# Rotating images by 90 degrees: the last four slabs turned in pairs, and a new order of stores

## Chip, cores, metric

One Trainium2 chip, one core. The metric is device time in microseconds (us) of one execution, the median of several runs. "Faster" or "slower" is said of differences over 2%; this study is about differences of a few tenths of a per cent, so each kernel is compared with runs of the kernel before on the same chip, with a 95% interval.

## The reference

```python
def setup_inputs():
    batch, c, h, w = 32, 3, 256, 256
    return {"x": np.random.randn(batch, c, h, w).astype(np.float32)}

def reference(x):
    return np.rot90(x, k=-1, axes=(-2, -1)).astype(np.float32)
```

96 images of 256x256 floats: 25.17 MB are read and 25.17 MB written, with no arithmetic.

## The kernel before

The images are cut into 12 slabs of 2.097 MB (8 images each), and a slab fills one unit of 16 KB in each of the 128 partitions. All slabs are loaded, turned by VectorE in 32x32 blocks, and stored when the loads are over. Slab n is turned into the unit that slab n-1 has left; slab 0 goes to PSUM and is copied back by ScalarE (ACT) at the end.

A slab that is turned alone has long rows (16 KB, 16 image rows, as one DMA packet) on one of its two sides only. `short` and `long` are the two cuts of the image rows:

```python
    def short(rows):
        return rows.rearrange("(n i p r) w -> n p i (r w)", i=I, p=P, r=RS)        # RS = 8: 8 KB runs

    def long(rows):
        return rows.rearrange("(n i m r) w -> n i m (r w)", i=I, m=P // I, r=RL)   # RL = 16: 16 KB runs
    ...
    long_st = (0, 1, 2, last)          # loaded in 8 KB, stored in 16 KB; the others the other way round
    for n in range(n_slabs):           # loads
        if n in (1, 2):
            ld = nc.sync.dma_start(out=units[n], in_=ld_short[n])
            continue
        for i in range(I):
            if n in long_st:
                ld = nc.sync.dma_start(out=units[n][:, i], in_=ld_short[n][:, i])
            else:
                ld = nc.sync.dma_start(out=units[n][i::I].rearrange("p i f -> p (i f)"), in_=ld_long[n, i])
            if (n, i) == (last, 0):
                mark = ld              # the first store waits for this load
    ...
    for n in range(n_slabs):           # turn, then store
        t_in, t_out = units[n], units[n - 1] if n else turned0
        ...                            # two transposes of 128x2048 elements
        if n in range(5, last):
            nc.sync.dma_start(out=st_short[n], in_=t_out)         # 2 MB, 256 packets of 8 KB
        elif n:
            for i in range(I):
                st = store(n, t_out, i)                           # 1 MB each
                ...
```

## Time and profile before

| | before |
|---|---|
| median, 3 runs | 123.8 us (123.74 to 123.87) |
| span of the profiled run | 121.9 us |
| VectorE busy | 92.9 us (76%) |
| DMA queue | 5248 packets (4608 of data), 98.1% busy |

The span is what the profiler sees between the first and the last instruction; the time of a run is about 1.9 us longer. The lines of the profile that carry this are shown in the prediction. Beside the page and its views I use the packet records of the trace: start, duration and bytes of every DMA packet. In the records a packet and the next one on its engine overlap, mostly by 3 or 4 ns.

### The profile page before, as it was taken

The page shows a single profiled execution, that of the slowest core. Times are in us where ns is not written, and L with a number is a line of the kernel's source. Part 1 is how long each engine was busy: PE and PEld are TensorE (multiplying, and loading weights), DVE is VectorE, ACT ScalarE, POOL GpSimd, SP SyncE. Part 2 cuts the span into 40 slices and gives each one's busy share as a digit, 9 for nine tenths or more (in the row PEclk, how much of TensorE's full clock was granted, in tenths as well). Part 3 has the DMA queues.
Part 4 walks back from the last instruction along what each step waited for, and adds up shares of the span by engine and source line. Part 5 has one row for each costly group of instructions (what it writes and reads, how often), then busy time and mean ns, then how long its engine had stood idle before and what let it go on. Part 6 is the DMA issues. An engine that isn't in the chain of part 4 may idle for free.

```text
span 121.9 us, 137 instructions
## 1 busy us (share of the span) xinstructions
DVE 92.9 (76%) x24; ACT 4.9 (4%) x3; POOL 0.2 (0%) x4
## 2 busy tenths in 40 slices
DVE  0039999999999999999999999999999992000000
ACT  0000000000000000000400000000000007400000
POOL 0000000000000000000000000000000000000000
DMA  3999999999999999999999999999999999999994
GB/s 86 430 430 430 427 433 430 430 430 430 430 430 430 430 430 430 430 430 390 427 468 430 430 390 430 430 430 430 411 419 419 427 419 419 414 427 473 425 419 188
DMA packets 5248, 50.33 MB, mean 413 GB/s; under 512 B 640, under 2 KB 640, under 8 KB 640
## 3 DMA queue, kind: packets, MB, share of 16 engines
q1 hardware_dynamic: 5248, 50.33, 98.1%
HBM read 25.17 MB, written 25.17 MB: 413 GB/s over the span
## 4 chain that ended last, share of the span: by engine, by line
DVE 44%; issue 29%; DMA 6%; DVEq 3%; ACT 2%; ACTq 1%; SPq 0%
DVE u L98 26%; DVE u L92 12%; DVE turned L92 6%; DMA u<-in_x_dram 6%; DVEq L138 3%; ACT u L110 2%; ACTq L138 1%; SPq L73 0%; DVEq L92 0%
## 5 line engine op out<-in xcount | busy, mean ns | idle before, releaser
L98 DVE STREAM_TRANSPOSE u<-u 128x2048 f32<-128x2048 f32 x16 | 62.4, 3947 | 0.3
L92 DVE STREAM_TRANSPOSE u<-u 128x2048 f32<-128x2048 f32 x6 | 23.4, 3984 | 0.1
L92 DVE STREAM_TRANSPOSE turned<-u 128x2048 f32<-128x2048 f32 x2 | 7.1, 3586 | 8.1 <-DMA u<-in_x_dram 8.1
L110 ACT COPY u<-turned 128x2048 f32<-128x2048 f32 x2 | 3.6, 1869 | 40.5 <-DVE u L92 40.5
L110 ACT ACT_TABLE_LOAD x1 | 1.3, 1283 | 59.6 <-DMA u<-in_x_dram 59.6
L127 POOL MEMSET const-bfloat16-1.0<- 128x1 bf16 x1 | 0.1, 102 | 0.0
L127 POOL MEMSET const-uint8-127<- 128x1 uint8 x1 | 0.1, 102 | 0.0
L127 POOL MEMSET const-float32-0.0<- 128x1 f32 x1 | 0.1, 99 | 0.2 <-issue 0.2
L127 POOL MEMSET const-float32-1.0<- 128x1 f32 x1 | 0.1, 99 | 0.0
## 6 DMA issues: line engine op xcount, KB each, us to landing
u<-in_x_dram SPq DMA_DIRECT2D x20, 1024.0 KB, 19.6
out_dram<-u SPq DMA_DIRECT2D x12, 1024.0 KB, 12.1
out_dram<-u SPq DMA_DIRECT2D x6, 2048.0 KB, 20.9
u<-in_x_dram SPq DMA_DIRECT2D x2, 2048.0 KB, 13.5
```

The lines of the kernel that those rows point to most:

```text
L92: nc.vector.transpose(out=dst[:, cs], in_=src[:, cs])
L98: nc.vector.transpose(out=dst[:, cs], in_=src[:, cs])
L110: nc.scalar.copy(out=units[last][:, i], in_=turned0[:, i])
L127: nc = _bacc.Bacc("TRN2", target_bir_lowering=False, num_devices=1)
L138: with _tile.TileContext(nc) as tc:
```

## The change

Its intent: a slab alone can have 16 KB packets on one side only, but two slabs that are turned together can have them on both. Slabs 8 and 9, and 10 and 11, become such pairs. A pair needs two free units at once, so stores must have left one by then: the stores of slabs 3 to 7 come first (4 at the very front, because the pair 8/9 goes into the units of slabs 3 and 7), then 1 and 2, then the pairs. Cut to its core:

```diff
-    long_st = (0, 1, 2, last)
+    long_st = (0, 1, 2)
+    both = (8, 10)
+    adjacent = [(3, 7), (8, 9), (10, 11)]          # units that lie side by side in one tile
...
-    for n in range(n_slabs):
+    for n in (0, 1, 2, 3, 7, 4, 5, 6, *range(8, n_slabs)):          # loads
...
+        elif n in paired:
+            src = pairs[both.index(n) + 1].rearrange("p a (r g c) -> p c r g a", r=RL, c=RL)
+            dst = pairs[both.index(n)].rearrange("p i (c k r) -> p c r k i", c=RL, r=RL)[:, :, ::-1, ::-1, :]
+            parts, step = 4, RL // 4
...
+        if n in paired:
+            for i in range(I):
+                nc.sync.dma_start(out=st_long[n, i], in_=pairs[both.index(first)][n - first :: I, i])
...
-        if n in range(5, last):
-            nc.sync.dma_start(out=st_short[n], in_=t_out)
+            return nc.sync.dma_start(out=st_short[n], in_=fours(home[n]))     # slabs 3 to 7, 2 MB each
...
+    for n in range(both[0]):
+        turn(n)
+    for n in (4, 3, 5, 6, 7, 1, 2):
+        st = store(n)
+    for n in range(both[0], n_slabs):
+        turn(n)
+        store(n)
```

So 1024 packets of 8 KB (the load of slab 11 and the stores of slabs 8, 9 and 10) become 512 of 16 KB.

## The prediction

> **What bounds the kernel now.** The kernel reads 25.17 MB and writes 25.17 MB through one DMA queue, and VectorE turns 32x32 blocks in between. I read the page first: the busy shares, the 40 slices, the queue.
>
> ```profile
> span 121.9 us, 137 instructions
> DVE 92.9 (76%) x24; ACT 4.9 (4%) x3; POOL 0.2 (0%) x4
> DMA  3999999999999999999999999999999999999994
> DMA packets 5248, 50.33 MB, mean 413 GB/s; under 512 B 640, under 2 KB 640, under 8 KB 640
> q1 hardware_dynamic: 5248, 50.33, 98.1%
> ```
>
> The 16 DMA engines are busy 98.1% of the span, with no thin slice but the first and the last; VectorE is at 76%. The page's chain that ended last gives VectorE 44%, but followed in order of time it stops with the ACT copies at 105.0 us, with 17 us still to go: that chain explains when the last buffers became ready, not what filled the time. So the transfers are the bound, and a gain can come from only three places: bytes (unchanged), empty time of the queue, or time per byte. Empty time is 1.9% of 121.9 = 2.3 us, of which the packet records of the trace put 1.76 us before the first packet and 1.2 us after the last (start and finish of the program; a little overlap of packets makes up the difference). In between there is no gap over 15 ns on an engine once the first microsecond of packets is past. There is no empty time to win. What is left is time per byte.
>
> The rate by stage, asked of the windows view with borders that I took from the packet records at whole slabs (a slab is 2.097 MB; columns: stretch, its length, busy time of three engines, clock, DMA share, GB/s):
>
> ```profile
> 17.20:56.34 39.14, 38.97 (x11) 0.00 (x0) 0.00 (x0) 1.00 1.01 429
> 56.34:61.31 4.97, 4.97 (x2) 1.28 (x1) 0.00 (x0) 1.00 1.01 422
> 61.31:71.05 9.74, 9.67 (x4) 0.00 (x0) 0.00 (x0) 1.00 1.01 431
> 71.05:110.71 39.66, 30.22 (x8) 3.63 (x2) 0.00 (x0) 1.00 1.01 423
> ```
>
> These are: loads of slabs 3 to 10 in 16 KB packets (429 GB/s); load of slab 11 in 8 KB packets (422); stores of slabs 1 and 2 in 16 KB packets (431); stores of slabs 3 to 10 in 8 KB packets (423). So 8 KB packets cost between 1.6% and 1.9% more per byte, in a queue that is full throughout. The packet records say the same by packet: a 16 KB packet takes 614 ns as a load and 611 to 618 ns as a store; an 8 KB packet takes 309 to 316 ns. Within the 8 KB stores it is not constant: slabs 3 and 4 (issued as 1 MB halves) average 309 ns, slab 5 311, slabs 6 to 10 313 to 316. I have no cause for that drift and carry it as an uncertainty.
>
> **What the Trainium skill says.** "DMA: Bandwidth & Descriptors", section Bandwidth (Where 436 GB/s comes from), puts the ceiling of the 16 engines at the SBUF ports at 435.2 GB/s. The trace agrees: its best stage moves 431. An estimate with that figure: 50.33 MB take no less than 115.6 us, and the 119 us from the first packet to the last are within 3% of that, so no packet shape can win more than about 3%. The same section (Why small descriptors are slow) gives each packet a fixed overhead of about 3 cycles; from its 850 MHz that is an estimated 3.5 ns. The trace's fastest 8 KB packets agree (2 x 309 - 614 = 4 ns saved per merged pair); the slower stores do not (2 x 314 - 614 = 14 ns), so most of the effect here is something else. "SBUF — State Buffer", section Door 1, says that a block of 64 neighbouring partitions reaches only half of the ports; the changed transfers take every second partition of 128, which by its table reaches all 16. The trace agrees: slabs 1 and 2 leave the chip in that form, and at 431 GB/s.
>
> **The change part by part.**
>
> Packets. Slab 11 is now loaded as 16 KB packets, and slabs 8, 9 and 10 are now stored so (slab 11 already was). A slab is 256 packets of 8 KB or 128 of 16 KB. So 4 x 256 = 1024 packets of 8 KB become 512 of 16 KB. On the critical resource that is worth:
> - load of slab 11: 2.097 MB at 422 is 4.97 us, at 429 it is 4.89: 0.08 us.
> - stores of slabs 8 to 10: by the packet records these three take 4.97, 4.98 and 4.98 us = 14.93. At the 4.87 us of slabs 1 and 2 they would take 14.61, at the 4.93 us (16 x 2 x 308 ns per engine) of the two slabs stored last they would take 14.79: 0.14 to 0.32 us. I take 0.25.
> - all of it lies on the path that sets the end, since the queue is never empty: 0.33 us together.
> - slabs 3 and 4 lose their 1 MB halves and become 2 MB transfers like slab 5 to 7. If the halves are why they ran at 309 ns and not at 313, that gives back 2 x 16 x 4 ns = 0.13 us. I take half, 0.06 us.
> - transfers go from 40 to 41; each posts 16 tiny packets of 9 ns, one per engine: 0.01 us.
>
> VectorE. 24 transposes stay 24, each of 128x2048 elements. The groups view of before has two quite different patterns within 1% of one another, so the third pattern (two slabs at once) should cost the same 3.95 us:
>
> ```profile
> L98 DVE STREAM_TRANSPOSE u<-u 128x2048 f32<-128x2048 f32 x16 | 62.4, 3947 | 0.3
> L92 DVE STREAM_TRANSPOSE u<-u 128x2048 f32<-128x2048 f32 x6 | 23.4, 3984 | 0.1
> L92 DVE STREAM_TRANSPOSE turned<-u 128x2048 f32<-128x2048 f32 x2 | 7.1, 3586 | 8.1 <-DMA u<-in_x_dram 8.1
> ```
>
> VectorE waits only 8.1 us for the first slab and never again. After the change: slab 0 from 8.1 to 15.2; slabs 1 to 7 at 7.83 us each to 70.0; pair 8/9 to 85.7; pair 10/11 to 101.4, where it ended before too. The one new wait is that pair 8/9 is turned into the units that slabs 4 and 8 would have had, so it needs the store of slab 4 landed.
>
> Order of stores. I lay the new order on the queue. Loads end at 61.31 - 0.08 = 61.2. Store of slab 4 is done at 66.2, so VectorE, free at 70.0, does not wait (slack 3 us). Slabs 4, 3, 5, 6, 7 at 4.96 us end at 86.0; slabs 1 and 2 at 95.8. Slabs 8 and 9 are needed then and ready at 85.7: slack 10 us. They last until 105.5, and 10 and 11 are ready at 101.4: slack 4.1 us, less about 1 to 1.7 us that a transfer needs from issue to its first packet (1.03 us for the first load). 10 and 11 last to about 115.3, and the ACT copies of slab 0 are ready at 101.4 + 3.6 = 105.0. So the new order costs nothing, and was needed only because a pair becomes ready at once.
>
> **Sum.** -0.33 + 0.06 + 0.01 = -0.26 us, with a hair more if 16 KB stores hold the 431 of slabs 1 and 2. Measured time 123.8 - 0.3 = 123.5 us.
>
> **The rivals.**
> 1. A gap between loads and stores. In the wait view of SyncE the first store waits for the landing of the first half of slab 11:
>
> ```profile
> SPq L81 <- DMA u<-in_x_dram: 16.8, 1, 16.8
> ```
>
> By the timeline it is issued at 59.6 us, and the last load packets end at 61.31: 1.7 us to get a store going, against 1.03 us measured for the first load. After, the second half is 16 KB packets and ends 0.05 us sooner, and the first store is a 2 MB transfer, whose issue takes SyncE 0.43 to 0.71 us as a load against 0.34 to 0.42 for a 1 MB one. So some 0.3 us of slack remain. For it: it is thin. Against it: before showed no gap there at all. It would make the time 123.6 to 124.0.
> 2. VectorE becomes late for the last pair (two-slab pattern slower, or a wait on the store of slab 4). For it: a pair's stores cannot start until all 4 pieces are turned, so the slack is 4 us instead of 9 before. Against it: the 8 pieces of both pairs would have to be 8% slower to use up even 2.5 us. Beyond that each lost microsecond is a microsecond of time: 10% slower transposes would give about 124.1.
> 3. The size of packets is not what makes slabs 8 to 10 slow, but their place late in the run (the drift). Then only the 4 ns per pair remain: 32 pairs per engine x 4 ns = 0.13 us, and the time is 123.7. Its mirror: the slowness grows with the number of 8 KB stores in a row, so fewer of them gain a bit more, 123.2.
>
> **Range and chances.** All outcomes with an intact queue lie between 123.2 and 123.75, and runs of one kernel spread by 0.13 us. A hand-over gap may add some tenths. I give 123.1 to 123.85 for 8 in 10. 2% is 2.5 us: nothing in the packets can win it (all stores and loads at 431 would save under 1.5 us), and losing it needs the queue dry for 2.8 us: 2%. Within 2%: 97.5%. Faster: 0.5%.
>
> **What would show it.** Packets other than tiny ones down from 4608 to 4096; queue share still near 98%; span 121.6. Load of slab 11 near 429 GB/s, stores of slabs 8 to 10 near 428 to 431, stores of slabs 3 to 7 near 423; VectorE 24 pieces of 3.95 us ending at 101.4 with no wait but the first. I am wrong if a slice in the middle falls below 9 tenths, if VectorE waits for a store, or if 16 KB stores late in the run take over 625 ns.

## The result, and the profile after

Measured: 123.27 us (median of 6 runs, 123.18 to 123.42) against 123.84 us for the kernel before in the same rounds: ratio 0.9955, 95% interval 0.9942 to 0.9967. Ratios here are the mean time of one kernel's runs over that of the other's runs of the same rounds, so not quite the ratio of the medians. That is 0.57 us less, same within 2% as forecast and inside the range, but about twice the 0.3 us that I had summed.

The page of the changed kernel, for the lines that answer to those of before:

```profile
span 121.5 us, 134 instructions
DVE 90.6 (75%) x24; ACT 4.9 (4%) x3; POOL 0.2 (0%) x4
DMA  3999999999999999999999999999999999999994
DMA packets 4752, 50.33 MB, mean 414 GB/s; under 512 B 656, under 2 KB 656, under 8 KB 656
q1 hardware_dynamic: 4752, 50.33, 97.9%
```

4752 packets less the 656 tiny ones are the 4096 foreseen. The queue is still full in every slice but the first and the last. VectorE is 2.3 us less busy. The groups and the waits of VectorE (after):

```profile
L116 DVE STREAM_TRANSPOSE u<-u 128x2048 f32<-128x2048 f32 x22 | 83.5, 3866 | 0.3
L116 DVE STREAM_TRANSPOSE turned<-u 128x2048 f32<-128x2048 f32 x2 | 7.1, 3586 | 8.2 <-DMA u<-in_x_dram 8.2
```
```profile
DVE turned L116 <- DMA u<-in_x_dram: 8.2, 1, 8.2
```

VectorE waits for the first load and for no store. Now the rate by stage. The first fence is the changed kernel, slabs 5 to 7 (8 KB stores) and then slabs 8 to 11 (16 KB stores); the second is the kernel before, slabs 5 to 7 and slabs 8 to 10, both 8 KB stores:

```profile
71.12:85.82 14.70, 14.67 (x5) 0.00 (x0) 0.00 (x0) 1.00 1.01 430
95.58:115.24 19.66, 3.56 (x1) 3.63 (x2) 0.00 (x0) 1.00 1.01 428
```
```profile
80.78:95.80 15.02, 14.95 (x5) 0.00 (x0) 0.00 (x0) 1.00 1.00 419
95.60:110.72 15.12, 5.77 (x2) 3.63 (x2) 0.00 (x0) 1.00 1.01 420
```

The last column is GB/s; a window counts whole packets by their start, so one row of 16 packets more or less is worth 2% of a window of 15 us with 8 KB packets and 4% with 16 KB ones, and such a number alone decides nothing here. The packet records do. This table gives, for each slab, how long one engine is occupied with its sixteenth of it: number of packets times (mean duration less 3 ns of overlap), in us.

| slab | before | after |
|---|---|---|
| load of 11 | 4.97 | 4.89 |
| stores of 1, 2 | 4.87, 4.87 | 4.87, 4.87 |
| stores of 3, 4 | 4.90, 4.90 | 4.90, 4.90 |
| stores of 5, 6, 7 (8 KB in both) | 4.93, 4.96, 5.00 | 4.90, 4.90, 4.90 |
| stores of 8, 9, 10 (8 KB, then 16 KB) | 4.97, 4.98, 4.98 | 4.88, 4.89, 4.88 |
| stores of 11, 0 | 4.91, 4.91 | 4.89, 4.90 |

The differences: load of 11, -0.08; stores 8 to 10, -0.27; stores 5 to 7, -0.20; 11 and 0, -0.03; the rest, 0.01. Together -0.57 us. Three fifths of that is packet size where I expected it. One third is in slabs 5 to 7, whose packets have the same size as before. The medians of the runs differ by 0.57 us too, but that the two agree to the last digit is luck: the table comes from one profiled execution of each kernel, and the spans of these two differ by only 0.42 us (121.93 and 121.50). What the table leaves out varies from profile to profile by as much as the parts in question: the load of slab 0 from 5.10 to 5.51 us, and the time from the end of the last data packet to the end of the span from 1.16 to 1.42 us.

The records show how slabs 5 to 7 differ. In the kernel before, every 8 KB store packet takes exactly 309 ns from 75 to 78 us. Then a growing share takes longer: a quarter of the packets by 81 us, half by 90 us, 85% by 101 us, and the mean is then 314 ns. In the changed kernel nearly all packets of slabs 3 to 7 are at 309 ns. Slow packets come there too, but later (a quarter of them by 93 us), when the 16 KB stores run: 611 ns undisturbed, 614 on average in the last 20 us, and 616 to 617 for the 16 KB stores that end the kernel before. A packet that is slow costs about the same surcharge **whatever its size**: between 95 and 110 us the 8 KB packets over 309 ns are on average 6.3 ns over it (kernel before), and the 16 KB packets over 611 ns 6.6 ns over it (changed kernel). So 16 KB packets pay it half as often per byte.

The growing share is a growing number of engines. The records do not name the engine, but each packet can be strung onto the engine whose last packet ended as it began. Then in the changed kernel, between 100 and 105 us, seven of the 16 engines have no slow packet at all, one has 3 of 8, and eight have 75 to 88%; in the kernel before all 16 have 75 to 94% by then. Engines turn slow at different times and then mostly stay so.

### The profile page after: what moved, and what is told of

It is laid out like the page before. It is cut to its first block, busy times and chain, and to the rows that moved or that the text cites. A ratio compares the mean times of both kernels' runs of the same rounds, so it can differ in the third digit from the quotient of the medians.

```text
span 121.5 us, 134 instructions
## 1 busy us (share of the span) xinstructions
DVE 90.6 (75%) x24; ACT 4.9 (4%) x3; POOL 0.2 (0%) x4
## 2 busy tenths in 40 slices
DMA packets 4752, 50.33 MB, mean 414 GB/s; under 512 B 656, under 2 KB 656, under 8 KB 656
## 3 DMA queue, kind: packets, MB, share of 16 engines
q1 hardware_dynamic: 4752, 50.33, 97.9%
## 4 chain that ended last, share of the span: by engine, by line
DVE 59%; issue 13%; DMA 6%; DVEq 3%; ACT 2%; ACTq 1%; SPq 0%
DVE u L116 53%; DVE turned L116 6%; DMA u<-in_x_dram 6%; DVEq L169 3%; ACT u L141 2%; ACTq L169 1%; SPq L92 0%; DVEq L116 0%
## 5 line engine op out<-in xcount | busy, mean ns | idle before, releaser
L116 DVE STREAM_TRANSPOSE u<-u 128x2048 f32<-128x2048 f32 x22 | 83.5, 3866 | 0.3
```

Source lines behind the costliest of these rows:

```text
L116: nc.vector.transpose(out=dst[:, h * step : (h + 1) * step], in_=src[:, h * step : (h + 1) * step])
```

## The experiments

The question was what the two parts of the change, larger packets and new order, contribute, and why slabs 5 to 7 became quicker. Size theory: all is packets. Order theory: the new order keeps the 8 KB stores undisturbed. Twelve kernels ran, all with the correct result, in three groups of four; those of one group shared their runs of the kernel before. Nine of the ten runs of the kernel before that stand against the second group (quarters, all_halves, after_halves, four_pairs) are those of the first, on the same chip; the third group (after_again, same_packets, eight_in_row, four_pairs2) ran on another chip. The edits below are cut to their core. "Records" is the change against the kernel before in the sum of the table above (load of 11 and all stores).

| run | median us | ratio to before (95% interval) | records, us | slabs 5 to 7 | slabs 8 to 10 |
|---|---|---|---|---|---|
| order_only | 123.71 | 0.9996 (0.9982 to 1.0009) | -0.18 | 4.90 | 4.96 to 4.97 |
| split_8k | 123.49 | 0.9975 (0.9963 to 0.9988) | -0.28 | 4.90 | 4.94 to 4.97 |
| early_1_2 | 123.23 | 0.9955 (0.9942 to 0.9967) | -0.62 | 4.90 to 4.91 | 4.87 to 4.88 |
| no_halves | 123.92 | 1.0010 (0.9997 to 1.0022) | -0.01 | 4.91 to 5.01 | 4.97 to 4.98 |
| quarters | 124.03 | 1.0013 (0.9999 to 1.0027) | +0.04 | 4.93 to 4.98 | 4.99 |
| all_halves | 123.87 | 1.0006 (0.9994 to 1.0019) | -0.14 | 4.90 to 4.95 | 4.98 |
| after_halves | 123.55 | 0.9976 (0.9964 to 0.9989) | -0.55 | 4.90 | 4.89 to 4.90 |
| after_again | 123.25 | 0.9948 (0.9935 to 0.9961) | -0.58 | 4.90 | 4.88 to 4.90 |
| same_packets | 123.75 | 0.9990 (0.9977 to 1.0002) | -0.27 | 4.90 | 4.92 to 4.98 |
| eight_in_row | 123.68 | 0.9986 (0.9974 to 0.9999) | -0.20 | 4.90 to 4.91 | 4.91 to 4.98 |

(four_pairs and four_pairs2 are told apart below.) An interval is some 0.15 us to either side, so a difference of 0.1 us between two rows is not shown.

### order_only: the new order, with the old packets

```diff
+    held = [turn(n) for n in range(8)]
+    for n in (4, 3, 5, 6, 7, 1, 2):
+        st = put(n, held[n])          # 3 to 10 as one 2 MB transfer each, the others as before
+    for n in range(8, n_slabs):
+        put(n, turn(n))
```

> The kernel before with one part of the change alone: slabs 4, 3, 5, 6, 7 are stored first (each as one 2 MB transfer), then 1 and 2, then 8 to 11; every packet keeps the size it had before. Size theory (the gain is the 1024 packets of 8 KB that became 512 of 16 KB): 123.8 us, and the 8 KB stores of slabs 5 to 7 still average some 313 ns a packet. Order theory (the new order keeps the 8 KB stores at the undisturbed 309 ns that they show throughout in the changed kernel): about 0.2 to 0.3 us faster than before, 123.5 to 123.6, with slabs 3 to 7 at 309 ns; what slabs 8 to 10 do is open.

Measured 123.71 us; the interval holds no change. The two windows are slabs 3, 5 and 6 and then slabs 8 to 10 of this kernel:

```profile
66.26:80.96 14.70, 14.63 (x5) 0.00 (x0) 0.00 (x0) 1.00 1.01 428
95.66:110.58 14.92, 5.95 (x2) 3.63 (x2) 0.00 (x0) 1.00 1.01 422
```

In the records the order theory is right about slabs 3 to 7 (all at 309 ns, 4.90 us a slab, 0.2 us gained), but slabs 8 to 10 are as slow as before. The order alone is worth 0.18 us in the records, and not clearly anything in the time.

### split_8k: the changed kernel with slabs 8 to 10 stored in 8 KB packets

```diff
+                if n != last:
+                    to, frm = (t.rearrange("m (h f) -> m h f", h=2)[:, ::-1] for t in (to, frm))
```

> The changed kernel with everything as it is (pairs, units, order, number of transfers), except that the stores of slabs 8 to 10 are cut into 8 KB packets again (the two halves of each row swapped on both sides, so that they are not merged). Size theory: those three slabs cost 48 x 2 x 309 to 314 ns instead of 48 x 2 x 306.5 per engine, 0.24 to 0.36 us... by my first estimate 0.2 to 0.3 us slower than the changed kernel: 123.5 to 123.6. Order theory: within 0.1 us of the changed kernel, 123.3, since the order is kept; slabs 3 to 7 at 309 ns in either case.

Measured 123.49 us, 0.26 us above early_1_2 of the same group (whose packets are those of the changed kernel). In the records slabs 8 to 10 go from 4.88 to 4.94, 4.97 and 4.97 us, 0.22 us together. The five runs of each do not overlap (123.44 to 123.59 and 123.21 to 123.33), and early_1_2 runs in the time of the changed kernel, so the size of the packets of slabs 8 to 10 is worth about 0.25 us by itself: against the changed kernel the edit touches nothing else but the order of the two halves of a row. No cost of that order is seen: the swapped packets take 312 to 314 ns, the unswapped ones of the kernel before 314.

### early_1_2: the changed kernel with slabs 1 and 2 stored early

```diff
-    for n in (4, 3, 5, 6, 7, 1, 2):
+    for n in (4, 1, 2, 3, 5, 6, 7):
```

> The changed kernel with the stores in the order 4, 1, 2, 3, 5, 6, 7: the pairs and all packet sizes as in the changed kernel, slabs 1 and 2 again near the front. Size theory: 123.3 us, equal to the changed kernel. Order theory: the 8 KB stores of slabs 3 to 7, now later, drift up towards 313 ns as before, which costs 4 slabs x 16 x up to 4 ns = up to 0.25 us: 123.4 to 123.5.

Measured 123.23 us, as the changed kernel. Slabs 5 to 7 move at the same place in the run as in the kernel before (81 to 96 us) and stay at 4.90 to 4.91 us, where before they had 4.93 to 5.00. So a late place is not enough to slow them, and the order theory as I had put it falls. That rests on one profiled execution, but all five runs of this kernel lie within 0.12 us.

### no_halves and all_halves: 1 MB or 2 MB transfers

```diff
-        if n in range(5, last):
+        if n in range(3, last):       # no_halves: slabs 3 to 10 as one 2 MB transfer each
+        if n in ():                   # all_halves: slabs 3 to 10 in two of 1 MB
```

> The kernel before with one edit: slabs 3 and 4 are stored as one 2 MB transfer each instead of two of 1 MB. My prediction charged up to 0.13 us for that (0.06 in the sum): 123.85 to 123.95. If the halves have nothing to do with the 309 ns that slabs 3 and 4 show, 123.8, and slabs 3 and 4 stay at 309 ns. If, the other way round, it is the change from halves to 2 MB that starts the drift, slabs 5 to 7 come down to 309 ns and the time to 123.6.

> The kernel before with one edit: slabs 5 to 10 are stored in two transfers of 1 MB as slabs 3 and 4 are, so no store has 256 packets. Burst theory: bursts about half as high (128 packets, up to 30 ns), 0.05 to 0.15 us faster than before, 123.65 to 123.75, on one line with the version that has no halves (123.92) and the kernel before (123.8). Rival (halves do not matter, the 0.1 us was noise): 123.8.

Measured 123.92 and 123.87 us against 123.8. Both intervals hold 1 (no change), and the two edits are opposite, so no effect of the number of halves on the time is shown. The records of no_halves keep slabs 3 and 4 at 309 ns in 2 MB form: what I charged for the halves (0.06 us) was not paid in their packets. Its median is 0.12 us up all the same, and its profile has 0.14 us more after the last data packet (1.30 us for 1.16). With halves throughout, slabs 5 and 6 stay quick (4.90) and slab 7 does not (4.95).

### quarters: late stores issued in small pieces

In the traces of the first group something else caught the eye. When slabs 9 and 10 are stored in 2 MB transfers of 256 packets, issued as soon as VectorE is done (85.7 and 93.5 us), about 1.3 us later the packets in flight on most engines become 20 to 50 ns longer, once. I took these bursts for what starts the slow phase, and cut the late transfers.

```diff
+            for q in range(4 if n >= 8 else 0):
+                nc.sync.dma_start(out=st_short[n][q % 2 :: 2, q // 2], in_=t_out[q % 2 :: 2, q // 2])
```

> The kernel before with one edit: the stores of slabs 8, 9 and 10, which are issued late (77.9, 85.7, 93.5 us) while slabs 5 to 7 are moving, are cut into four transfers of 64 packets each instead of one of 256; order and packet size stay. Burst theory (in the traces so far many engines' packets become 20 to 60 ns longer about 1.3 us after such a late issue of 256 or 128 packets, and from then on most packets are a few ns slow; issues of 64 packets do not do it): no packet more than 18 ns over 309 after 85 us until the 16 KB stores, slabs 5 to 7 at 309 to 310 ns, 0.15 to 0.3 us faster than before, 123.5 to 123.65. Rival (the slow packets come from late 8 KB stores as such or from the place in the run): 123.8, slabs 5 to 7 at 311 to 316.

Measured 124.03 us, if anything slower. The bursts are gone: nothing between 75 and 99 us is more than 20 ns over 309. But the packets are as slow as ever. The window is slabs 5 to 7 of this kernel:

```profile
80.93:95.84 14.91, 14.84 (x5) 0.00 (x0) 0.00 (x0) 1.00 1.01 421
```

The burst theory falls: without the bursts the slow phase comes as before. Whether a late issue of any size plays a part is not tested.

### after_halves: the changed kernel with slabs 3 to 7 in halves

```diff
-            return nc.sync.dma_start(out=st_short[n], in_=fours(home[n]))
+            for i in range(I):
+                st = nc.sync.dma_start(out=st_short[n][:, i], in_=fours(home[n])[:, i])
```

> The changed kernel with slabs 3 to 7 stored in halves of 1 MB. All of them are issued before 82 us and run at 309 ns already, so both theories: 123.27, within 0.06. If it is 0.1 or more faster, the 2 MB form costs something even without bursts, and my sum was right to charge for it.

Measured 123.55 us: a miss, 0.28 us above the changed kernel (which ran in another group), though the packets are as quick as there (the mean over the engines ends at 120.19 us, in the changed kernel at 120.21). But the last packets of the 16 engines end between 120.10 and 120.48 us, where the changed kernel has 120.15 to 120.30: one engine or a few came late. An end is set by the slowest engine, and the mean of the packets does not show that. The stragglers are half of it: the profiled run is the slowest of the six (123.68), its span is 0.40 us longer, 0.19 of that is the later end of the last data packet, and 0.21 comes after it (1.42 us for 1.21). Why this form has stragglers is open, and so is the other half.

### after_again and same_packets: the control, and the changed kernel with the old packets

```diff
+                if n == last:         # same_packets: split_8k, and the load of slab 11 cut in the same way
+                    to, frm = (t.rearrange("m (h f) -> m h f", h=2)[:, ::-1] for t in (to, frm))
```

> The changed kernel once more, unedited, as the control of this group of runs: 123.27 within 0.1 us.

> The changed kernel with the packets of the kernel before: the load of slab 11 and the stores of slabs 8 to 10 are cut into 8 KB packets again (4608 data packets as before), while pairs, units, order and transfers stay. Size theory, all of the gain is packets: 123.8. If the two terms of my sum are right (0.25 for the stores, 0.08 for the load) and the rest is something else (slabs 5 to 7 stored in the quiet first part of the stores): 123.27 + 0.33 = 123.6, and 0.2 us of the gain remain.

The control came to 123.25 us. With the packets of before, but the new order, units and pairs, the time is 123.75 us, 0.50 us more than the control and no longer clearly below the kernel before. In the records the difference is 0.31 us (load of 11 from 4.89 to 4.97; slabs 8 to 10 from 4.88, 4.90 and 4.89 to 4.92, 4.97 and 4.98; slabs 11 and 0 0.02 more); the load of slab 0, which varies from run to run, and the noise of the medians make up the rest (0.17 us for that load in the two profiled runs). Slabs 5 to 7 are quick here as well. So packet size is most of the gain: without it 0.1 us (order_only, same_packets, eight_in_row: 0.05, 0.12 and 0.17 us by their ratios), with it 0.57. The 0.20 us that slabs 5 to 7 gain in the records is thus not clearly shown in the time: of these three intervals only that of eight_in_row leaves out 1, and barely.

### eight_in_row: all eight 8 KB slabs first

```diff
+    for n in (4, 3, 5, 6, 7):
+        st = put(n, held[n])
+    for n in (8, 9, 10):
+        put(n, turn(n))
+    for n in (1, 2):
+        put(n, held[n])
```

> The kernel before, all packets as before, with the eight slabs that are stored in 8 KB packets first, in one row (4, 3, 5, 6, 7, 8, 9, 10) and then 1, 2, 11 and 0. Quiet-start theory (the first 20 to 25 us of the stores are quiet, then most packets cost some 4 ns more, whatever their size): slabs 4, 3, 5, 6, 7 at 309 ns, the next three at 311 to 314, 123.6 to 123.75. Rival (the slowness grows with the number of 8 KB stores in a row): already the fourth and fifth are above 311. Rival (what counts is how late a store is issued before it moves): slabs 9 and 10, issued just in time, are the slow ones, and 1 and 2 behind them stay at 306 or less.

Measured 123.68 us. Slabs 4 to 8 have 4.90 to 4.91 us, slabs 9 and 10 4.96 and 4.98, and slabs 1 and 2 behind them are not at 4.87 but at 4.91. The slowness does not follow the number of 8 KB stores in a row from its start, and once it is there it takes the 16 KB packets too. When it comes differs: a quarter of the packets are slow by 81 us in the kernel before and in quarters, by 88 in order_only, 90 here, 93 and 96 in the two profiled runs of the changed kernel, 98 in same_packets and 106 in early_1_2. Each is from one execution, and two executions of one kernel differ by 3 us. I can say what the slow phase costs, and not what starts it.

### four_pairs and four_pairs2: more pairs

If packets are what counts, pair slabs 1 and 2 and slabs 3 and 4 as well: one unit is still free when they are turned, because the last slabs are not loaded yet.

```diff
+    slot = dict(zip(range(n_slabs), "ABCDEFGHIJEK"))   # four_pairs: where each slab is loaded (four_pairs2: ...IJDE)
+    home = {5: "D", 6: "F", 7: "G"}                    # four_pairs2: 5 goes to K
+    to = {1: "AX", 3: "BC", 8: "HD", 10: "IJ"}         # four_pairs2: 8 goes to HK
```

> The change carried further: slabs 1 and 2 and slabs 3 and 4 are turned in pairs too, into a unit that stays free because slab 10 is loaded last, into a unit that the pair 3 and 4 has left. Loads of slabs 1 and 2 and stores of 3 and 4 become 16 KB packets: another 512 of 8 KB merged to 256... in all 4 slabs' sides, 1024 packets to 512. Size theory: loads 2 x 16 x (310 - 307) = 0.1 us, stores 2 x 16 x (309 - 306) = 0.1 us per engine, so 0.2 us faster than the changed kernel, 123.05 to 123.1. Rival: VectorE starts the second step later (it needs slabs 1 and 2 both, at about 18 us) and the last load waits for VectorE at about 47 us; if either empties the queue, slower than 123.3.

Measured 153.82 us, some 30 us too slow (the text of four_pairs2 below says 28). The waits of SyncE, which issues all transfers:

```profile
SPq L92 <- DVE uBC L111: 31.8, 1, 31.8
```

and of VectorE:

```profile
DVE uBC L111 <- DMA uHDEK<-in_x_dram: 25.0, 1, 25.0
```

Units H, D, E and K shared one tile, and VectorE's turn of slabs 3 and 4 (in D and E) waited for every load into that tile that stood ahead of it in the program, those of slabs 7 and 11 among them; the load of slab 10 waited for that turn. No data packet is in flight for 16.5 us, and three shorter holes of 2.7 to 6.8 us follow among the stores. That is a build fault, and says nothing on packets. Mended:

> The change carried further, mended: slabs 1 and 2, 3 and 4, 8 and 9, 10 and 11 in pairs; slabs 10 and 11 are loaded into the two units that the pair 3 and 4 leaves, and no two units share a tile unless both are needed at once (the first try lost 28 us because its tile of four units made the turn of 3 and 4 wait for the loads of 7 and 11). 3584 data packets. Size theory: 0.2 us faster than the changed kernel, 123.05 to 123.1; VectorE waits about 2.7 us for slab 2 and has its pair 10 and 11 done at about 100 us, no later than the changed kernel's by over 2 us; the load of slab 10 is issued at about 47 us with 3 us to spare. If either empties the queue: slower than 123.3.

Measured 123.69 us, ratio 0.9981 (0.9970 to 0.9993): better than the kernel before, 0.44 us worse than the control with 512 fewer packets. The loads did gain: the stores begin at 61.3 us on the mean of the engines, against 61.45 and 61.39 in the two profiled runs of the changed kernel. From there to the end of the last data packet the stores lost some 0.4 us (59.2 us against 58.8). SyncE's waits and the windows of slabs 5, 6 and the next one:

```profile
SPq L115 <- DVE uG L111: 7.4, 1, 7.4
```
```profile
61.10:71.00 9.90, 9.83 (x4) 0.00 (x0) 0.00 (x0) 1.00 0.98 416
71.00:76.00 5.00, 5.00 (x2) 0.00 (x0) 0.00 (x0) 1.00 1.02 426
```

I had put the store of slab 7 third. It waits for VectorE until 70.2 us, and all stores behind it in SyncE's order wait with it, while the two stores ahead of it last only until 71. In the changed kernel four stores, 20 us, stand ahead of the one that waits. With the queue nearly dry, the slow phase begins at about 71 us (a quarter of the packets and more at once, where the changed kernel has that at 93), the packets of the stores cost 0.19 us more in the records, and eight engines show one gap of 0.12 to 0.25 us near 71 us. Whether the gap starts the slow phase, or only comes at the same time, is not shown. Whether the four pairs with slab 7 stored later would win is not tried.

These two kernels also show the transposes of the pairs apart (groups of four_pairs2):

```profile
L111 DVE STREAM_TRANSPOSE uHK<-uIJ 128x2048 f32<-128x2048 f32 x4 | 14.4, 3680 | 0.0
L111 DVE STREAM_TRANSPOSE uF<-uG 128x2048 f32<-128x2048 f32 x2 | 7.8, 3966 | 0.0
```

A piece of a pair takes 3.68 us, a piece of a single slab 3.95 to 3.97.

## Why the prediction was right, and where it was not

- **The number.** 123.27 us lies inside the range, but a range of 123.1 to 123.85 held "no change" as well, so that shows little. The term that was mis-sized is that of the stores of slabs 5 to 7, left at nothing and measured at 0.20 us (below). The number also lies near the 123.2 given to the mirror of rival 3 (slowness that grows with the number of 8 KB stores in a row); that is luck, as eight_in_row speaks against it.
- **The bound.** Right. The queue stays full, and the time follows the packets.
- **Load of slab 11, 0.08 us.** Right: 0.08 in the records. same_packets differs from split_8k in this load alone, by 0.08 in the records again (4.97 and 4.89); they ran in different groups, and their ratios (0.9990 and 0.9975) agree within the noise.
- **Stores of slabs 8 to 10, 0.25 us.** Right: 0.27 in the records, and about 0.25 by split_8k.
- **Slabs 3 and 4 without halves, +0.06 us.** Not paid in the packets: both stay at 309 ns. In the kernel before, the same edit alone was 0.12 us slower, which its interval does not tell from nothing.
- **"Stores of slabs 3 to 7 near 423."** Here the sum failed: it had no term for slabs 5 to 7, because their packets do not change. They gave 0.20 us, from a mean of 313 ns to 309. The term was mis-sized at nothing, because I had carried the drift as an uncertainty of my number and not as something that the change could move. With these two corrected the sum of 0.26 becomes 0.52, and 0.02 more from slabs 8 to 10 and 0.03 from slabs 11 and 0 lead to the 0.57 us of the records.
- **Rival 3.** It said that, if place and not size makes the late stores slow, only 4 ns per merged pair would be won. That was too simple. Late stores of both sizes turn slow, but by 6 to 7 ns per slow packet, so a merged pair saves one such surcharge on top. "DMA: Bandwidth & Descriptors" in the Trainium skill (Bandwidth, Why small descriptors are slow) speaks of a fixed cost per packet, and that is the shape of it; the 3.5 ns that the prediction estimated from it fit the quiet phase alone (two packets of 309 ns against one of 611, less one overlap of 3 ns: 4 ns).
- **Rival 1, the gap at hand-over.** Not seen: slice by slice the queue is full, and the load packets are followed at once by store packets.
- **Rival 2, VectorE too late.** It was the other way: pairs took 3.68 us a piece and not 3.95, and VectorE ended near 99 us instead of 101.4, off the path in any case.
- **Two sums.** The 4.93 us for the slabs stored last leave out the overlap that the other figures take off; with it they are 4.91, and the low end of the term for slabs 8 to 10 is 0.20 us, not 0.14. And all transfers at 431 GB/s would save about 2.2 us from the first packet to the last (119.0 less 116.8), not under 1.5; that is still under 2%.
- **Open.** What makes an engine turn slow. Not the number of 8 KB stores in a row, not the size of late transfers (quarters), and not the place in the order alone (early_1_2). No run settles it.

## What to carry to other kernels

When the DMA queue is full from end to end, only the time per packet is left to win, and it is small: halving the number of packets for a sixth of the bytes gave 0.35 us of 124 in the records. Before adding up a sum, ask of every drift in the records whether the change can move it; here a third of the gain in the records came from transfers whose packets it did not touch. And lay the stores so that the one that waits for an engine has many microseconds of others ahead of it: everything behind it in the issuing engine's order waits with it.

## What the Trainium skill lacked or had wrong

- "DMA: Bandwidth & Descriptors", Bandwidth: one overhead per packet. The runs show two phases with the same transfers: 309 ns for every 8 KB store packet and 611 for 16 KB ones, and later, engine by engine, packets that are 6 to 7 ns slower in either size (means of 314 and 614 to 617); the page has nothing on the second.
- The same page, Rules for kernel authors: for the most bandwidth, at least 1 MiB per DMA. With many transfers queued the runs show little of that: the kernel before with late stores in quarters (0.5 MB), halves and wholes lies within 0.23 us (123.8 to 124.03).
- "VectorE: DVE Perf Modes", The three transpose paths: the section has one VectorE duration, for 128x128 bf16, none for 32-bit elements, and nothing on access patterns. 128x2048 32-bit elements took 3.59 us into PSUM, 3.68 us for pairs and 3.95 to 3.99 us for single slabs.
- No page has how far the ends of the engines lie apart when one queue feeds them all: 0.15 us in the changed kernel (120.15 to 120.30), 0.38 in after_halves (120.10 to 120.48), with the same mean per packet.
